# FFN 1's down projection by seven products of block sums in place of eight, in turns with up units, and three weight buffers for four

## The chip, the cores and the metric

The kernel runs on one core of a Trainium2 chip. A core has a matrix engine (PE, with its weight loads PEld), a vector engine (DVE), a scalar engine (ACT), a third elementwise engine (POOL), a queue that issues DMAs (SP), an on-chip memory in 128 partitions, and eight banks in which PE accumulates. Every engine works through its own instructions in the order of the program and waits for the others by semaphores. The metric is the device time of one execution in microseconds (us); less is better. A ratio is time after over time before.

## The reference

A decoder trunk of two layers over 256 tokens of width 2048, all in float32: pooling mixer, layer norm, gated FFN with a causal convolution of width 3, layer norm; then attention, layer norm, the second FFN (FFN 1, of layer 1), layer norm. What the change touches is the last line of the FFN:

```python
D_MODEL = 2048
SEQ = 256
D_FF = 128 * ((8 * D_MODEL // 3 + 127) // 128)   # 5504
...
def conv_ffn(h, w_up, conv_w, conv_b, w_down):
    """Gated MLP with causal depthwise conv (width 3) between up-projection and activation."""
    S = h.shape[1]
    u = h @ w_up
    up = jnp.pad(u, ((0, 0), (CONV_WIDTH - 1, 0), (0, 0)))
    c = conv_b + up[:, 0:S] * conv_w[0]
    for j in range(1, CONV_WIDTH):
        c = c + up[:, j:j + S] * conv_w[j]
    gate, val = jnp.split(c, 2, axis=-1)
    return (jax.nn.silu(gate) * val) @ w_down
...
        h = layer_norm(DEEPNORM_ALPHA * h + ff, ln2_g[i], ln2_b[i])
```

The output is the stream after the last layer norm, 256 x 2048.

## The kernel before, in words

**Units.** All weights pass through one list, `units`, of 364 entries. A unit is a tile of up to 512 rows by 512 columns of a weight (1 MB), the matmuls that use it, and what is to be done when its group is complete. `run_units` takes them in the list's order; the order of that list, and nothing else, sets the order of the program on every engine. For unit i it calls `ahead(i)`, then issues the unit's matmuls, then runs what is due (`later(n, fn)` puts a step off by n units), then the unit's own end (`post`).

**Loading and splitting.** `ahead(i)` issues loads on SP up to unit i + 5 (`do_load`; three buffers named `raw`), and splits up to unit i + `SP_AHEAD` (`do_split`). A split makes two rounded parts of a float32 weight: ACT casts `raw` to `wh` (L76), DVE subtracts to get `wl` (L77). Both have `SP_AHEAD + 1`, that is four, buffers. Each product is then three: high with high, high with low, low with high. The activations are split in the same way (`split_act`: L206 on ACT, L202 on DVE, in tiles called `xc`, `xp` or `g` with both parts).

**FFN 1.** Units 232 to 363. The inner width of 5504 is eleven pieces of 512 (the last of 384), q = 0 to 10. For each q there are four up units of the gate half and four of the value half (one for each 512 rows of the input). Most have 16 blocks, each with one matmul of 512 columns (L135) and one of 256 (L136). When a half's four units are done, `evac` copies and adds their sums (L512 on ACT, L513 on DVE), `conv` does the convolution (L521 on ACT, L525 on DVE), and the product of both halves becomes `g[q]` (L538, L539, L560, L206, L202). The down projection (`down`, `group_tm`) runs in chunks of q: 0 to 2, 3 to 5, 6 and 7, 8 to 10. A chunk is four groups, one for each 512 columns of the output, and in a group one unit for each q, of 24 matmuls of 512 columns (L165 to L167): two token halves, four blocks of 128 rows, three products. A group's two sums are added to the residual `ht` by DVE (L612). The up units of a chunk all come before its down units. `turns` swaps one pair of neighbours at each group's edge.

**What the change touches:** `SP_AHEAD` (L25), `do_load`, `do_split`, `ahead`, `run_units`, `group_tm`'s use for q below 8, `val_chain`, and the loop at the end of `ffn` (L590 to L593).

## Time and profile before

| | |
|---|---|
| time, three runs | 2086.20 to 2086.56 us, median 2086.37 |
| the profiled execution | 2086.31 us, of which the span of its instructions is 2084.5 |
| granted PE clock, mean | 0.998 |
| matmuls | 12992 |
| weights read | 380 MB at 183 GB/s |

The span is the time from the first to the last instruction. The profile gives busy time by engine, by group of instructions (line, engine, operation, tiles written and read, shape; then count, busy us, mean ns of one, and the idle time of the engine just before them with what ended it), the waits, the chain of work that ended last, and a timeline of single instructions. Matmuls are pipelined: a length in the timeline reaches beyond the next one's start, so what a matmul costs is read from start to start.

### The profile page before, as it was taken

What the parts mean: (1) busy time and instruction counts of PE and PEld (TensorE: products, weight loads), DVE (VectorE), ACT (ScalarE), POOL (GpSimd) and SP (SyncE); (2) the same over time, 40 slices, a digit from 0 to 9 for tenths busy, and PEclk for the clock granted to TensorE, in tenths of its full rate; (3) what the DMA queues carried; (4) which work ended last, traced back from release to release, by engine and by line L of the source; (5) the groups of instructions that cost most, each with busy time, mean ns of one, the idle gap of its engine ahead of it and who ended that gap; (6) DMA issues with size and microseconds to landing.
All of it is one profiled execution on the core that took longest, in us unless ns stands there. A gap on an engine that the chain in (4) does not pass through costs nothing.

```text
span 2084.5 us, 30605 instructions
## 1 busy us (share of the span) xinstructions
PE 2066.8 (99%) x12992; PEld 1861.9 (89%) x12992; DVE 1396.6 (67%) x1719; ACT 1027.4 (49%) x1142; POOL 11.4 (1%) x38
## 2 busy tenths in 40 slices
PE   9999999999999999999999999999999999999997
PEld 9999998888888888899888889999888888888886
DVE  6757787756756766778755666686646664665676
ACT  6445665345534535556544434475535543544552
POOL 2000000000000000000000000000000000000000
PEclk9999999999999999999999999999999999999999
DMA  8655465555565565554555455546555555555453
GB/s 263 211 184 186 156 204 180 202 182 185 179 202 182 182 202 172 187 188 162 182 172 176 164 173 185 182 143 202 189 195 182 183 197 186 183 193 190 153 202 131
DMA packets 195304, 384.09 MB, mean 184 GB/s; under 512 B 7022, under 2 KB 15876, under 8 KB 194912
## 3 DMA queue, kind: packets, MB, share of 16 engines
q1 hardware_dynamic: 194240, 381.71, 55.1%
q8 instruction: 101, 1.65, 0.3%
q0 software_dynamic: 928, 0.44, 0.1%
q14 instruction: 35, 0.29, 0.0%
HBM read 380.01 MB, written 2.10 MB: 183 GB/s over the span
## 4 chain that ended last, share of the span: by engine, by line
PE 98%; DVE 1%; DMA 0%; SPq 0%; ACT 0%; issue 0%
PE acc L135 35%; PE acc L136 18%; PE acc L139 9%; PE acc L140 9%; PE acc L138 9%; PE t L165 5%; PE t L166 5%; PE t L167 5%; PE s L720 0%; PE o L760 0%; DMA raw<-in_pool_w_in_dram 0%; PE pT L747 0%; PE s L719 0%; PE o L761 0%; PE hT L603 0%; DVE ht L669 0%
## 5 line engine op out<-in xcount | busy, mean ns | idle before, releaser
L77 DVE TENSOR_TENSOR wl<-raw,wh 128x2048 fp32r<-128x2048 f32 (+2 forms) x376 | 821.8, 2188 | 534.5 <-ACT wh L76 524.5
L76 ACT CAST wh<-raw 128x2048 fp32r<-128x2048 f32 (+2 forms) x376 | 685.6, 1827 | 609.6 <-PE acc L135 297.7
L135 PE MATMUL acc<-xc,wh 128*128 128x512 f32 x2624 | 924.1, 396 | 0.0
L136 PE MATMUL acc<-xc,wl 128*128 128x256 f32 x2624 | 736.2, 281 | 0.0
L135 PEld LDWEIGHTS acc<-xc,wh 128*128 128x128 f32 x2624 | 495.0, 189 | 116.6
L136 PEld LDWEIGHTS acc<-xc,wl 128*128 128x128 f32 x2624 | 494.9, 189 | 0.2
L135 PE MATMUL acc<-g,wh 128*128 128x512 f32 x512 | 179.9, 396 | 0.0
L138 PE MATMUL acc<-xc,wh 128*128 128x256 f32 x512 | 144.5, 282 | 1.6 <-ACT wh L76 1.6
L140 PE MATMUL acc<-xc,wl 128*128 128x256 f32 x512 | 144.4, 282 | 0.2 <-DVE wl L77 0.2
L139 PE MATMUL acc<-xc,wh 128*128 128x256 f32 x512 | 144.1, 281 | 0.0
L136 PE MATMUL acc<-g,wl 128*128 128x256 f32 x512 | 143.6, 280 | 0.0
L525 DVE SCALAR_TENSOR_TENSOR c<-u,cv,c 128x256 f32<-128x256 f32 x344 | 141.9, 480 | 0.6
L165 PE MATMUL t<-wh,g 128*128 128x512 f32 (+1 forms) x355 | 137.9, 388 | 0.0
L166 PE MATMUL t<-wl,g 128*128 128x512 f32 (+1 forms) x355 | 137.3, 387 | 0.0
L167 PE MATMUL t<-wh,g 128*128 128x512 f32 (+1 forms) x355 | 137.3, 387 | 0.0
L135 PEld LDWEIGHTS acc<-g,wh 128*128 128x128 f32 x512 | 96.6, 189 | 22.8
L139 PE MATMUL acc<-xp,wh 128*128 128x258 f32 x384 | 109.2, 284 | 0.0
L138 PE MATMUL acc<-xp,wh 128*128 128x258 f32 x384 | 109.0, 284 | 0.0
L140 PE MATMUL acc<-xp,wl 128*128 128x258 f32 x384 | 107.9, 281 | 0.0
L512 ACT COPY ut<-acc 128x256 f32<-128x256 f32 x140 | 51.6, 372 | 96.2 <-PE acc L136 96.0
L138 PEld LDWEIGHTS acc<-xc,wh 128*128 128x128 f32 x512 | 97.2, 190 | 1.8 <-ACT wh L76 1.8
L140 PEld LDWEIGHTS acc<-xc,wl 128*128 128x128 f32 x512 | 96.4, 188 | 0.5 <-DVE wl L77 0.4
(203 smaller groups left out, 2812.7 us busy)
## 6 DMA issues: line engine op xcount, KB each, us to landing
raw<-in_ffn_w_up_dram SPq DMA_DIRECT2D x160, 1024.0 KB, 5.1
raw<-in_ffn_w_down_dram SPq DMA_DIRECT2D x80, 1024.0 KB, 5.0
raw<-in_pool_w_out_dram SPq DMA_DIRECT2D x16, 1024.0 KB, 5.0
raw<-in_shared_w_k_dram SPq DMA_DIRECT2D x16, 1024.0 KB, 5.0
raw<-in_attn_w_q_dram SPq DMA_DIRECT2D x16, 1024.0 KB, 5.0
raw<-in_shared_w_v_dram SPq DMA_DIRECT2D x16, 1024.0 KB, 5.0
raw<-in_attn_w_o_dram SPq DMA_DIRECT2D x16, 1024.0 KB, 5.1
raw<-in_pool_w_in_dram SPq DMA_DIRECT2D x12, 1024.0 KB, 5.6
```

The costliest lines, as they stand in the source:

```text
L76: A.copy(wh[i][:, s], r[:, s])
L77: V.tensor_tensor(wl[i][:, s], r[:, s], wh[i][:, s].bitcast(F32), OP.subtract)
L135: PE.matmul(ps[m], h[:, k, c], q[:, k, :, :T], start=st, stop=False)
L136: PE.matmul(ps[m][:, :T], l[:, k, c], q[:, k, 0, :T], start=False, stop=sp)
L138: PE.matmul(ps[m][:, :n], h[:, k, c], q[:, k, 0, :n], start=st, stop=False)
L139: PE.matmul(ps[m][:, :n], h[:, k, c], q[:, k, 1, :n], start=False, stop=False)
L140: PE.matmul(ps[m][:, :n], l[:, k, c], q[:, k, 0, :n], start=False, stop=sp and not shifted)
L165: PE.matmul(to, xh, h[:, k, c], start=j == 0 and k == 0, stop=False)
L166: PE.matmul(to, xh, l[:, k, c], start=False, stop=False)
L167: PE.matmul(to, xl, h[:, k, c], start=False, stop=j == len(r0s) - 1 and k == nk - 1)
L512: A.copy(t, ps[m][:, T:])
L525: V.scalar_tensor_tensor(c[:, m, :], u[:, m, i:i + T], cv[:, i, j:j + 1], c[:, m, :], op0=OP.mult, op1=OP.add)
```

## The change

For layer 1 and q = 0 to 7, the product of a 512 by 512 weight tile with `g[q]` is now made as a 2 by 2 block product by seven block products instead of eight. The tile is cut in halves of rows and columns, `g[q]` in halves of its inner width and of tokens.

- **Two units for each tile.** `group_s` makes an "a" unit of three products and a "b" unit of four. Each product has two blocks of 128 rows and three matmuls of 256 columns: 18 and 24. Only a has a load; b has none and uses a's tile.
- **Splits.** For a, ACT casts three of the four blocks in two pieces (L103 of the new program), DVE subtracts (L105) and then forms four block sums in place in `raw` (L107 to L110). For b, ACT casts the four sums (L97) and DVE subtracts (L98). `split_order` puts the next unit that isn't a b ahead of each b in the order of splits; `ahead` splits in that order until all that are wanted are done.
- **Activation sums.** `val_chain` forms four sums of blocks of `g[q]` into `pend` (L289 to L292); `sums_tile` splits them into `xsum` (L295 on ACT, L296 on DVE) ahead of the chunk's first a.
- **Results.** Four banks hold the partial sums of a group; `s_post` combines them into `ht` with one copy on ACT (L819) and eight instructions on DVE (L820 to L828).
- **Order.** q = 0 and 1 up; then four turns, in which the eight pairs of q = a, a + 1 stand between the up units of the next two (in the last, three) q; then the down units of q = 8 to 10 as before.
- **Buffers.** `SP_AHEAD` is 2, so `wh` and `wl` have three buffers, in the whole kernel.

The diff, shortened to what it does:

```diff
 EPS = 1e-5
-SP_AHEAD = 3
+SP_AHEAD = 2
 WARM = 5
...
     state = {"loaded": 0, "split": 0, "done": 0}
+    is_split, order = set(), []
     raw, wh, wl = {}, {}, {}
...
         src = units[i][0]
+        if src is None:
+            return
         nk, n = src.shape[0] // P, src.shape[1]
...
     def do_split(i):
+        kind = units[i][3] if len(units[i]) > 3 else None
+        if kind is not None:
+            return split_sums(i, kind)
         r = raw.pop(i)
...
+    B1, B2, N1, N2 = slice(0, 2), slice(2, 4), slice(0, 256), slice(256, 512)
+    def split_sums(i, kind):
+        h = wh[i] = wp.tile([P, 4, 512], F32R, name=f"wh{i}", tag="wh")
+        l = wl[i] = wp.tile([P, 4, 512], F32R, name=f"wl{i}", tag="wl")
+        if kind == "b":
+            r = raw.pop(i - 1)
+            A.copy(h, r)
+            V.tensor_tensor(l, r, h.bitcast(F32), OP.subtract)
+            return
+        r = raw[i]
+        parts = [(slice(0, 4), N1), (B2, N2)]
+        for k, n in parts:
+            A.copy(h[:, k, n], r[:, k, n])
+        for k, n in parts:
+            V.tensor_tensor(l[:, k, n], r[:, k, n], h[:, k, n].bitcast(F32), OP.subtract)
+        r11, r12, r21, r22 = r[:, B1, N1], r[:, B1, N2], r[:, B2, N1], r[:, B2, N2]
+        V.tensor_tensor(r11, r12, r11, OP.subtract)
+        V.tensor_tensor(r12, r22, r12, OP.subtract)
+        V.tensor_tensor(r22, r22, r11, OP.subtract)
+        V.tensor_tensor(r21, r21, r22, OP.subtract)
+    def split_order():
+        held = None
+        for i, u in enumerate(units):
+            if len(u) > 3 and u[3] == "b":
+                held = i
+                continue
+            order.append(i)
+            if held is not None:
+                order.append(held)
+                held = None
+        if held is not None:
+            order.append(held)
     def ahead(i):
+        if not order:
+            split_order()
         while state["loaded"] < min(len(units), i + LD_AHEAD + 1):
...
         n = max(0, min(i - 1, SP_AHEAD) if i > 2 else 0)
-        while state["split"] < min(len(units), i + n + 1):
-            do_split(state["split"])
+        want = set(range(min(len(units), i + n + 1)))
+        while not want <= is_split:
+            j = order[state["split"]]
+            do_split(j)
+            is_split.add(j)
             state["split"] += 1
...
                 fn()
-            _, mm, post = units[i]
+            mm, post = units[i][1:3]
             mm(wh.pop(i), wl.pop(i))
...
+    def group_s(w, qs, c0, xq, xs, post):
+        ps = []
+        def mk(j, q, kind):
+            def go(h, l):
+                if j == 0 and kind == "a":
+                    ps.extend([bank(f"s{i}") for i in range(4)])
+                x, y = xq(q), xs(q)
+                last = j == len(qs) - 1
+                def a(k, t):
+                    return lambda hl, kk: x[:, k + kk, hl, t * P:t * P + P]
+                def sm(i):
+                    return lambda hl, kk: y[:, hl, i, kk, :]
+                if kind == "a":
+                    prods = [(a(0, 0), 0, N1, 0, 0, True, False), (a(2, 0), 2, N1, 2, 0, True, False),
+                             (sm(3), 2, N2, 0, 1, False, True)]
+                else:
+                    prods = [(a(2, 1), 2, N1, 1, 0, True, False), (sm(0), 0, N1, 1, 1, False, True),
+                             (sm(1), 2, N2, 3, 0, True, True), (sm(2), 0, N2, 2, 1, False, True)]
+                for left, k0, n, b, half, begins, ends in prods:
+                    to = ps[b][:, 256 * half:256 * half + 256]
+                    for kk in range(2):
+                        st, sp = begins and j == 0 and kk == 0, ends and last and kk == 1
+                        PE.matmul(to, left(0, kk), h[:, k0 + kk, n], start=st, stop=False)
+                        PE.matmul(to, left(0, kk), l[:, k0 + kk, n], start=False, stop=False)
+                        PE.matmul(to, left(1, kk), h[:, k0 + kk, n], start=False, stop=sp)
+            return go
+        for j, q in enumerate(qs):
+            units.append((w[512 * q:512 * q + 512, c0:c0 + 512], mk(j, q, "a"), None, "a"))
+            units.append((None, mk(j, q, "b"), (lambda: post(ps)) if j == len(qs) - 1 else None, "b"))
+    def sums(dst, src):
+        a11, a12, a21, a22 = (src[:, k:k + 2, t * P:t * P + P] for k, t in ((0, 0), (2, 0), (0, 1), (2, 1)))
+        V.tensor_tensor(dst[:, 0], a21, a22, OP.add)
+        V.tensor_tensor(dst[:, 1], dst[:, 0], a11, OP.subtract)
+        V.tensor_tensor(dst[:, 2], a11, a21, OP.subtract)
+        V.tensor_tensor(dst[:, 3], a12, dst[:, 1], OP.subtract)
+    def sums_split(dst, src):
+        A.copy(dst[:, 0], src)
+        V.tensor_tensor(dst[:, 1], src, dst[:, 0].bitcast(F32), OP.subtract)
     def quad_tile(nm):
...
         w_up, w_dn = ffn_w_up[lay], ffn_w_down[lay]
-        gq, gates = {}, {}
+        gq, gates, pend, xsum = {}, {}, {}, {}
+        seven = 8 if lay == 1 else 0
...
                     split_act(gq[q], s[:, :nb])
+                    if q < seven:
+                        pend[q] = (hp if q % 2 else lnp).tile([P, 4, 2, P], F32, name="pend", tag="h" if q % 2 else "sq")
+                        sums(pend[q], s)
...
-        for a, b in ((0, 3), (3, 6), (6, 8), (8, 11)):
-            for q in range(a, b):
+        if lay == 0:
+            for a, b in ((0, 3), (3, 6), (6, 8), (8, 11)):
+                for q in range(a, b):
+                    up(q)
+                down(range(a, b), b == 11)
+            return
+        def sums_tile(q):
+            xsum[q] = pools["ffn"].tile([P, 2, 4, 2, P], F32R, name="xsum", tag="xsum", bufs=2)
+            sums_split(xsum[q], pend.pop(q))
+        def down_s(qs):
+            mark = len(units)
+            for c in range(4):
+                group_s(w_dn, qs, 512 * c, lambda q: gq[q], lambda q: xsum[q], s_post(c))
+            got = units[mark:]
+            del units[mark:]
+            return [got[i:i + 2] for i in range(0, len(got), 2)]
+        def ups(qs):
+            mark = len(units)
+            for q in qs:
                 up(q)
-            down(range(a, b), b == 11)
+            got = units[mark:]
+            del units[mark:]
+            return got
+        units.extend(ups((0, 1)))
+        for a in (0, 2, 4, 6):
+            us, ds = ups((a + 2, a + 3) if a < 6 else (8, 9, 10)), down_s((a, a + 1))
+            at = (4, 5, 7, 8, 10, 11, 13, 14) if a < 6 else (4, 5, 8, 9, 12, 13, 16, 17)
+            for i, u in enumerate(us):
+                if i == at[0] - 1:
+                    before.setdefault(len(units), []).extend([lambda q=q: sums_tile(q) for q in (a, a + 1)])
+                units.append(u)
+                for k, d in zip(at, ds):
+                    if k == i + 1:
+                        units.extend(d)
+        down(range(8, 11), True)
...
                 store(cc, 1)
+        return post
+    def s_post(c):
+        def post(ps):
+            fp = pools["ffn"]
+            y = HT[c]
+            p1, u2, u3 = (fp.tile([P, 256], F32, name=nm, tag="s3", bufs=3) for nm in ("p1", "u2", "u3"))
+            A.copy(p1, ps[0][:, :256])
+            V.tensor_tensor(y[:, 0, :], y[:, 0, :], ps[0], OP.add)
+            V.tensor_tensor(u2, p1, ps[3][:, :256], OP.add)
+            V.tensor_tensor(y[:, 0, :256], y[:, 0, :256], ps[2][:, :256], OP.add)
+            V.tensor_tensor(u3, u2, ps[2][:, 256:], OP.add)
+            V.tensor_tensor(u2, u2, ps[1][:, 256:], OP.add)
+            V.tensor_tensor(y[:, 1, :], y[:, 1, :], ps[1], OP.add)
+            V.tensor_tensor(y[:, 0, 256:], y[:, 0, 256:], u2, OP.add)
+            y2 = y[:, 1, :].rearrange("p (a n) -> p a n", a=2)
+            V.tensor_tensor(y2, y2, u3.unsqueeze(1).to_broadcast([P, 2, 256]), OP.add)
         return post
...
```

Where instructions stand now. **First place: ACT's casts in the first turn.** Before, in a down chunk, units 259 to 263 (the number behind `wh` and `raw` is the unit's; the one behind the underscore only counts tiles):

```order
L76 CAST wh259_14005<-raw259_13900 128x2048
L206 CAST g_14036<-c_13847 128x4x256
L76 CAST wh260_14041<-raw260_13938 128x2048
L76 CAST wh261_14071<-raw261_14003 128x2048
L76 CAST wh262_14103<-raw262_14039 128x2048
L76 CAST wh263_14135<-raw263_14069 128x2048
```

After the change, units 256 to 261, of which 257, 258 and 261 are up units, 259 is an a, and 256 and 260 are b units, which read the `raw` tile of 255 and 259:

```order
L84 CAST wh257_13900<-raw257_13823 128x2048
L97 CAST wh256_13904<-raw255_13693 128x2048
L84 CAST wh258_13964<-raw258_13860 128x2048
L819 COPY p1_13992<-s0_13825 128x256
L103 CAST wh259_14006<-raw259_13898 128x4x256
L103 CAST wh259_14006<-raw259_13898 128x2x256
L84 CAST wh261_14048<-raw261_13962 128x2048
L97 CAST wh260_14052<-raw259_13898 128x2048
```

The casts no longer stand in the order of the units: 257 is ahead of 256, and 261 ahead of 260. PE runs 256 to 261 in the order of their numbers.

**Second place: DVE in the first turn, around the second pair.** Before, the subtractions of units 255 to 258, with a convolution and a gate's product between them:

```order
L77 TENSOR_TENSOR wl255_13808<-raw255_13689,wh255_13807 128x2048
L525 SCALAR_TENSOR_TENSOR c_13847<-u_13791,cv1_733,c_13847 128x256 x8
L77 TENSOR_TENSOR wl256_13863<-raw256_13740,wh256_13862 128x2048
L539 TENSOR_TENSOR c_13847<-u_13791,c_13847 128x1024
L77 TENSOR_TENSOR wl257_13903<-raw257_13805,wh257_13902 128x2048
L77 TENSOR_TENSOR wl258_13941<-raw258_13860,wh258_13940 128x2048
```

After, from a gate's convolution to the split of unit 258; 255 is an a, 256 its b, 257 and 258 up units:

```order
L626 SCALAR_TENSOR_TENSOR c_13847<-u_13809,cv1_729,c_13847 128x256 x8
L105 TENSOR_TENSOR wl255_13863<-raw255_13693,wh255_13862 128x4x256
L105 TENSOR_TENSOR wl255_13863<-raw255_13693,wh255_13862 128x2x256
L107 TENSOR_TENSOR raw255_13693<-raw255_13693 128x2x256
L108 TENSOR_TENSOR raw255_13693<-raw255_13693 128x2x256
L109 TENSOR_TENSOR raw255_13693<-raw255_13693 128x2x256
L110 TENSOR_TENSOR raw255_13693<-raw255_13693 128x2x256
L640 TENSOR_TENSOR c_13847<-u_13809,c_13847 128x1024
L85 TENSOR_TENSOR wl257_13901<-raw257_13823,wh257_13900 128x2048
L98 TENSOR_TENSOR wl256_13905<-raw255_13693,wh256_13904 128x2048
L85 TENSOR_TENSOR wl258_13965<-raw258_13860,wh258_13964 128x2048
```

Between the convolution and the split of the next up unit now stand two subtractions and four block sums of the a, and the b's own subtraction comes behind the up unit's.

**Third place: DVE in the first turn, behind a value half's end** (numbers left out but for the weight tiles; the first row is the subtraction of b unit 263, `wl_14247` is that of up unit 265):

```order
L98 TENSOR_TENSOR wl_14155<-raw_14004,wh_14154 128x2048
L595 MEMSET u 128x4x2
L614 TENSOR_TENSOR u<-acc,ut 128x256 x4
L626 SCALAR_TENSOR_TENSOR c<-u,cv_729,c 128x256 x8
L661 TENSOR_TENSOR c<-c 128x1024
L302 TENSOR_TENSOR g<-c,g 128x4x256
L289 TENSOR_TENSOR pend<-c 128x256
L290 TENSOR_TENSOR pend<-pend,c 128x256
L291 TENSOR_TENSOR pend<-c 128x256
L292 TENSOR_TENSOR pend<-c,pend 128x256
L85 TENSOR_TENSOR wl_14247<-raw_14112,wh_14246 128x2048
L820 TENSOR_TENSOR ht<-ht,s_14090 128x512
```

The first row of `s_post` is the last shown; seven more follow, and then the split of a unit 266, of up unit 268 and of b unit 267. New in this piece are the four rows of `pend` and `s_post`; before, the subtractions of the next units followed the low part of `g` directly.

## Prediction

> **What bounds the kernel now.** I read the page's busy shares and its chain of work that ended last, then the waits of PE, then busy time by stage, then single rows of the timeline for what one step costs.
>
> ```profile
> span 2084.5 us, 30605 instructions
> PE 2066.8 (99%) x12992; PEld 1861.9 (89%) x12992; DVE 1396.6 (67%) x1719; ACT 1027.4 (49%) x1142; POOL 11.4 (1%) x38
> PE 98%; DVE 1%; DMA 0%; SPq 0%; ACT 0%; issue 0%
> ```
>
> The first two lines are the span and each engine's busy time, the third is the chain's share by engine. PE is on the chain for 98% of the span, so a microsecond of matmuls less is a microsecond less, as long as nothing makes PE wait. The next view, who waited for whom, kept to PE, has four rows of which this is the longest:
>
> ```profile
> PE acc L138 <- ACT wh L76: 1.6, 1, 1.6
> ```
>
> It is at the start. After that PE never waits: every split weight tile (`wh`, `wl`) is ready ahead of its unit. What the other engines have to spare in FFN 1 shows in two stretches, 24 up units, then 12 down units (columns: stretch, its length, busy time of PE, PEld, DVE, ACT, POOL, clock, DMA share, GB/s):
>
> ```profile
> 1549.00:1684.00 135.00, 135.00 (x770) 117.98 (x769) 87.36 (x101) 68.39 (x73) 0.00 (x0) 1.00 0.57 187
> 1684.00:1751.00 67.00, 67.00 (x290) 54.16 (x290) 38.42 (x31) 26.16 (x19) 0.00 (x0) 1.00 0.56 188
> ```
>
> DVE is busy 65% and 57% of them. So there is room on DVE, but not without end, and the change spends it.
>
> **The change part by part. 1: fewer products.** Matmuls of the timeline (start in us, length, engine, line, tiles, shape):
>
> ```profile
> 1311.17 0.28 PE L138 MATMUL acc<-o,wh 128*128 128x256 f32 x1
> ...
> 1339.69 0.29 PE L138 MATMUL acc<-xp,wh 128*128 128x258 f32 x1
> ...
> 1683.60 0.39 PE L165 MATMUL t<-wh,g 128*128 128x512 f32 x1
> ...
> 1750.57 0.39 PE L135 MATMUL acc<-xc,wh 128*128 128x512 f32 x1
> ```
>
> The first two rows bound five units of 48 matmuls of 256 columns: 28.52 us / 240 = 0.1188 us each. The other two bound twelve down units of 24 matmuls of 512 columns: 66.97 / 288 = 0.2325 us. An old down unit is 24 x 0.2325 = 5.58 us; the new pair is 18 matmuls ("a", 2.14 us) and 24 ("b", 2.85 us) of 256 columns, 42 x 0.1188 = 4.99 us. That is 0.59 us less for each of 32: **-18.9 us**. An up unit is 16 x (0.2325 + 0.1188) = 5.62 us; there are as many as before.
>
> **2: the wait for "b".** The three slots of `wh` are taken in the order of the splits, and that order is up, a, next up, b. In the rows of ACT shown with the change (258, 259, 261, 260) b's tile therefore takes the slot of the up unit that runs just before a: b's cast can't begin before a does. What follows then has rows in the trace before, where a cast also waited for the end of a unit (1627.40 is the next unit's first matmul):
>
> ```profile
> 1627.40 0.39 PE L135 MATMUL acc<-xc,wh 128*128 128x512 f32 x1
> ...
> 1627.49 1.91 ACT L76 CAST wh<-raw 128x2048 fp32r<-128x2048 f32 x1 [2.23 <-PE acc L135]
> ...
> 1629.42 2.29 DVE L77 TENSOR_TENSOR wl<-raw,wh 128x2048 fp32r<-128x2048 f32 x1 [1.98 <-ACT wh L76]
> ```
>
> From that matmul to the end of the subtraction are 4.31 us. Unit a covers 2.14 of them, and b's second matmul reads `wl`: PE stands about 2.2 us at every pair, with DVE free. The four-slot kernel hid the same 4.31 us behind three whole units. 32 x 2.2 = **+70.4 us**. No other work lies between a and b on PE, so nothing covers it.
>
> **3: more work on DVE.** What it costs, by rows of like shape, grouped and then in time:
>
> ```profile
> L77 DVE TENSOR_TENSOR wl<-raw,wh 128x2048 fp32r<-128x2048 f32 x111 | 254.3, 2291 | 184.3 <-ACT wh L76 183.7
> L513 DVE TENSOR_TENSOR u<-acc,ut 128x256 f32<-128x256 f32 x70 | 26.3, 417 | 18.1 <-ACT ut L512 18.1
> L612 DVE TENSOR_TENSOR ht<-ht,t 128x512 f32<-128x512 f32 x31 | 21.2, 683 | 14.7 <-PE t L167 14.7
> L202 DVE TENSOR_TENSOR g<-c,g 128x1024 fp32r<-128x1024 f32 x10 | 12.3, 1227 | 11.2 <-ACT g L206 11.2
> ```
>
> ```profile
> 1641.07 2.29 DVE L77 TENSOR_TENSOR wl<-raw,wh 128x2048 fp32r<-128x2048 f32 x1 [1.38 <-ACT wh L76]
> 1643.27 3.26 DVE L525 SCALAR_TENSOR_TENSOR c<-u,cv,c 128x256 f32<-128x256 f32 x8
> 1646.45 2.29 DVE L77 TENSOR_TENSOR wl<-raw,wh 128x2048 fp32r<-128x2048 f32 x1
> ...
> 2066.05 0.69 DVE L648 TENSOR_TENSOR ht<-ht,g 128x512 f32<-128x512 f32 x1 [0.88 <-ACT ht L645]
> 2066.77 0.69 DVE L649 TENSOR_TENSOR ht<-ht,b 128x512 f32<-128x512 f32 x1
> 2067.38 0.68 DVE L648 TENSOR_TENSOR ht<-ht,g 128x512 f32<-128x512 f32 x1
> ```
>
> An instruction begins before the last one ends, so I count from start to start: a whole split 2.20, a convolution of four blocks 3.18, a 512-column step 0.72 where it needs the one before (L649) and 0.61 where not. By the same 0.07 to 0.09 of overlap, 1024 columns (1227 ns) are 1.15 and 256 columns (417 ns) 0.35, or about 0.42 where they depend. The new steps then are: split of a, 1.15 + 0.61 + four dependent block sums of 512 = 4.6; split of b, 2.2; `s_post`, three of 512 and five of 256 = 3.7; four activation sums 1.7; the low part of a sum 1.15. No row shows subtractions in place on strided blocks. Ends for their 0.72: 0.61 (start to start of independent ones) and 1.15 (the next larger shape); I take L649, the nearest.
>
> A turn of 16 up units and 8 pairs is 16 x 5.62 + 8 x 4.99 = 129.8 us of PE. DVE has 16 x 2.2 + 8 x 6.8 + 4 groups x (4 x 0.35 + 3.18) + products and low parts of g 2 x 1.15 + 2 x 3.4 + sums 2 x 1.7 + 2 x 1.15 + 4 x 3.7 = 138 us. The 3.4 hold a wait for ACT's cast, 24.1 us over 22 times:
>
> ```profile
> DVE g L202 <- ACT g L206: 24.1, 22, 1.1
> ```
>
> So DVE needs more than the bare 129.8, but less than the 129.8 + 8 x 2.2 = 147.4 that part 2 makes of it. On average it fits; it is in bursts that it doesn't. I follow its queue, which is strictly in order, from the end of one b's subtraction to the next b's:
> - First pair: the third product of a reads `xsum`, whose low part stands behind b's subtraction in DVE's queue. PE stands 4.31 + 1.15 - 1.43 (two products) = 4.0 instead of 2.2: +1.8.
> - Second pair (the rows of DVE shown with the change): low parts 2.3, evacuation 1.4, convolution 3.18, split of a 4.6, gate product 1.15, split of the next up 2.2, split of b 2.2 = 17.0 us. From the same point PE has the rest of the first pair's a and b, an up unit and an a: 1.2 + 0.7 + 2.85 + 5.62 + 2.14 = 12.5. It stands 4.5: +2.3.
> - Fifth pair, behind a value group's end: evacuation 1.4, convolution 3.18, g 3.4, sums 1.7, split 2.2, `s_post` 3.7, split of a 4.6, two splits 4.4 = 24.6 us, against b, two ups and a on PE, 2.85 + 11.24 + 2.14 = 16.2. It stands 8.4 in two pieces, the first before the second up unit: +6.2.
> - The other five pairs find DVE done in time: 2.2 each.
>
> That is 10.3 us a turn beyond part 2. There are four turns (the last has 24 up units, and the same kinds of bursts): **+41 us**.
>
> **4: three buffers elsewhere.** A split made three units ahead is now made two ahead, at the same place in DVE's queue. Of 376 splits of the trace before, 246 were waited for by a DVE that had nothing else to do (us in total, times, longest):
>
> ```profile
> DVE wl L77 <- ACT wh L76: 524.5, 246, 5.4
> ```
>
> Those end as in part 2, 4.3 us after their buffer's release, and two units give 11.2: no cost. It is short at the two places where layer norm's work stands in the queue; there the subtraction in the slot of the unit after next ends too late for the unit itself:
>
> ```profile
> 266.38 0.28 PE L138 MATMUL acc<-xc,wh 128*128 128x256 f32 x1
> ...
> 266.92 2.29 DVE L77 TENSOR_TENSOR wl<-raw,wh 128x2048 fp32r<-128x2048 f32 x1
> ...
> 1387.69 0.28 PE L138 MATMUL acc<-xc,wh 128*128 128x256 f32 x1
> ...
> 1387.98 2.28 DVE L77 TENSOR_TENSOR wl<-raw,wh 128x2048 fp32r<-128x2048 f32 x1
> ```
>
> The unit that starts at 266.38 would get its `wl` at 269.21, the one at 1387.69 at 1390.26: 2.8 + 2.6 = **+5.4 us**. (Ends: nothing, if DVE's own waits shrink there; 11, if ACT's casts come late as well.)
>
> At nothing I cost ACT's added casts and copies (it is idle half the time, and b's cast is counted above), and the DMAs: SP's queue holds the same loads in the same order,
>
> ```profile
> raw<-in_ffn_w_down_dram SPq DMA_DIRECT2D x80, 1024.0 KB, 5.0
> ```
>
> and a load takes 5.0 us. A pair's raw tile is held until b's subtraction, but the load that follows into it is wanted two or three units later, 10 us or more; should that cover go in the fifth pair's burst, it is 2 us a turn.
>
> **Sum.** -18.9 + 70.4 + 41 + 5.4 = +98 us on the profiled execution's 2086.3 (span 2084.5 and 1.8 around it), which is within 0.1 of the median of 2086.37: **2184 us**.
>
> **The rivals.** *DVE's bursts are absorbed* (cheaper block sums, or slack that I don't see): parts 1, 2 and 4 alone, 2086 - 18.9 + 70.4 + 5.4 = 2143. For it: the sum over a turn fits. Against it: the order within the queue.
>
> *The clock falls in the waits.* In the trace it fell once, after PE's last matmul:
>
> ```profile
> 2070.03 0.28 PE L167 MATMUL t<-wh,g 128*128 128x256 f32 x1
> ...
> 2072.00:2078.00 6.00, 0.00 (x0) 0.00 (x0) 5.79 (x14) 0.29 (x1) 0.00 (x0) 0.69 0.11 44
> 2078.00:2084.00 6.00, 0.00 (x0) 0.00 (x0) 3.23 (x5) 0.00 (x0) 0.00 (x0) 0.50 0.45 175
> ```
>
> PE ends at 2070.3; a mean of 0.69 over six microseconds is 3.7 us at half clock, so it fell at 2074.3, 4.0 us after. Four waits in a turn are of 4.0 to 4.5 us, right at that. If each costs about 4 us at half clock, 2 us of work are lost: 16 x 2 = 32, some of which waits for DVE anyway: 2200 to 2216. The Trainium skill, "TensorE: Matmul & The Clock Gate", Part 1 on the HAM clock gate, speaks against the change in the same way: one idle window of about 3.4 us halves the clock, and about 3.4 us of activity bring it back. By its figure the long waits would nearly all do so, 16 x 1.7 = 27 us, an estimate, and the waits of 2.2 us would not. One fall in the tail can't tell the two figures apart.
>
> *Faster.* If b's cast were released one unit earlier, 4.31 us would hide behind an up unit and a (7.8 us), part 2 would be zero, and with DVE's 138 pressed under 130 the time would be 2086 - 18.9 + 5.4 = 2073. It decides from the point at which b's split ends within a's 2.14 us. The slot order speaks against it at every pair; only a release of the slot before the up unit's last matmul could make it so.
>
> *DVE costs more than I took*, with block sums nearer 1.15 than 0.72: 1.7 us more for each pair, all of it in the bursts and some elsewhere: 2200 to 2240.
>
> **How the numbers follow.** My forecast, 2184 (2160 to 2207): 0.6. Bursts absorbed, 2130 to 2160: 0.18. Clock or dearer DVE, 2207 to 2245: 0.18. Faster: 0.03; within 0.2%, which is about what a measurement of this kernel can tell from no change: 0.01. The range for 8 in 10 is 2138 to 2222: it leaves out the faster case and the ends of the two slow ones. Slower by over 0.2%: 0.96.
>
> **What would show it.** In the changed kernel's waits of PE, `s1` (b) waiting for `wl` of L98 should lead with some 32 waits and 70 us or more, most near 2.2 us; next `acc` and `s0` after the bursts. `s` matmuls should start every 0.119 us. If b's waits are much under 2 us, part 2 is wrong; if PE waits little beyond them, part 3 is; if the page's clock row shows 8s in the last third, the clock rival holds. DVE's share should come to some 75% of the span.

## The result, and the profile after

| | before | after |
|---|---|---|
| time, median of the runs | 2086.28 us (2085.94 to 2086.56) | 2219.51 us (2216.95 to 2223.23) |
| after / before | | 1.064 [1.0627, 1.0652] |
| profiled execution, its span | 2086.31, 2084.5 us | 2216.95, 2214.8 us |

The change makes the kernel 133 us slower. The page of the changed kernel, the lines that answer to those of before (span, busy times, the granted clock in 40 slices, the chain that ended last):

```profile
span 2214.8 us, 32282 instructions
PE 2101.1 (95%) x13568; PEld 1919.0 (87%) x13568; DVE 1596.8 (72%) x2055; ACT 1085.5 (49%) x1230; POOL 11.4 (1%) x38
PEclk9999999999999999999999999999998998999999
PE 80%; DVE 14%; ACT 4%; issue 2%; DMA 0%; SPq 0%; ACTq 0%; DVEq 0%
```

PE's share of the chain falls from 98% to 80%, and DVE and ACT come onto it. PE is busy 34 us *longer* than before, though the change takes 18.9 us of matmuls away. Both have to be explained. The waits of PE, one row for each awaited line:

```profile
PE s L278 <- DVE wl L98: 47.2, 22, 3.2
PE s L277 <- ACT wh L97: 18.1, 6, 5.2
PE s L278 <- DVE u L595: 11.7, 6, 1.9
PE s L279 <- DVE xsum L296: 8.1, 4, 2.0
PE s L277 <- ACT xsum L295: 4.9, 4, 1.5
PE acc L190 <- DVE wl L85: 4.3, 5, 1.3
```

L97 and L98 are b's cast and subtraction. The third row names a memset of 0.07 us that stands behind b's subtraction in DVE's queue; its six waits are of the same 1.94 us and belong to L98. Why b's split comes so late shows at the pair whose a begins at 1499.02, in the rows of PE, ACT and DVE:

```profile
1499.02 0.28 PE L277 MATMUL s<-wh,g 128*128 128x256 f32 x1
...
1499.15 1.91 ACT L97 CAST wh<-raw 128x2048 fp32r<-128x2048 f32 x1 [3.75 <-PE acc L185]
...
1501.09 2.29 DVE L98 TENSOR_TENSOR wl<-raw,wh 128x2048 fp32r<-128x2048 f32 x1 [3.36 <-ACT wh L97]
```

ACT stood idle for 3.75 us until the matmuls of the up unit ahead of a gave the slot free, and DVE is done 4.36 us after a's first matmul. Of the 30 casts of b before which ACT stood idle, 25 were released by an up unit (L185, L186) and five by DVE's last block sum (L110). The stretch of one turn, from the first pair of the second turn to that of the third:

```profile
1627.31:1790.98 163.67, 142.21 (x850) 128.45 (x849) 134.33 (x172) 77.45 (x82) 0.00 (x0) 0.93 0.46 155
```

A turn takes 163.7 us. PE stands for 163.67 - 142.21 = 21.5 of them, and is at work for 142.2, where its matmuls at full speed are 129.8. The granted clock, 0.93, says most of why. One b, matmul by matmul:

```profile
1501.14 0.36 PE L277 MATMUL s<-wh,g 128*128 128x256 f32 x1
1503.44 0.38 PE L278 MATMUL s<-wl,g 128*128 128x256 f32 x1 [1.94 <-DVE wl L98]
1503.66 0.28 PE L279 MATMUL s<-wh,g 128*128 128x256 f32 x1
...
1504.13 0.41 PE L277 MATMUL s<-wh,xsum 128*128 128x256 f32 x1
1504.34 0.42 PE L278 MATMUL s<-wl,xsum 128*128 128x256 f32 x1
```

```profile
1500.71:1504.12 3.41, 1.47 (x12) 1.26 (x11) 3.03 (x2) 1.91 (x3) 0.00 (x0) 1.00 0.44 170
1504.12:1507.53 3.41, 3.41 (x18) 3.41 (x17) 3.31 (x6) 0.00 (x0) 0.00 (x0) 0.50 0.89 286
```

The wait is 1.94 us. The first step behind it takes 0.22 us (1503.44 to 1503.66) where others take 0.12. Then, 0.7 us *after* PE had begun again, the clock halves for 3.41 us, and a matmul takes 0.21 us. So each wait costs more than it lasts.

### The profile page after: what moved, and what is told of

The parts are those of the page before. It is cut to its first block, busy times and chain, and to the rows that moved or that the text cites. A ratio compares the mean times of both kernels' runs of the same rounds, so it can differ in the third digit from the quotient of the medians.

```text
span 2214.8 us, 32282 instructions
## 1 busy us (share of the span) xinstructions
PE 2101.1 (95%) x13568; PEld 1919.0 (87%) x13568; DVE 1596.8 (72%) x2055; ACT 1085.5 (49%) x1230; POOL 11.4 (1%) x38
## 4 chain that ended last, share of the span: by engine, by line
PE 80%; DVE 14%; ACT 4%; issue 2%; DMA 0%; SPq 0%; ACTq 0%; DVEq 0%
PE acc L185 31%; PE acc L186 16%; PE acc L190 7%; PE acc L189 7%; PE acc L188 7%; DVE wl L98 3%; DVE wl L85 3%; PE t L216 2%; PE t L215 2%; PE t L217 2%; DVE c L626 2%; ACT wh L97 2%; PE s L278 2%; PE s L279 1%; PE s L277 1%
## 5 line engine op out<-in xcount | busy, mean ns | idle before, releaser
L85 DVE TENSOR_TENSOR wl<-raw,wh 128x2048 fp32r<-128x2048 f32 (+2 forms) x344 | 747.9, 2177 | 404.6 <-ACT wh L84 396.4
L185 PE MATMUL acc<-xc,wh 128*128 128x512 f32 x2624 | 927.2, 396 | 0.0
L84 ACT CAST wh<-raw 128x2048 fp32r<-128x2048 f32 (+2 forms) x344 | 624.3, 1819 | 531.4 <-PE acc L185 255.5
L186 PE MATMUL acc<-xc,wl 128*128 128x256 f32 x2624 | 737.1, 281 | 1.5 <-DVE wl L85 1.5
L185 PEld LDWEIGHTS acc<-xc,wh 128*128 128x128 f32 x2624 | 496.7, 189 | 115.4
L186 PEld LDWEIGHTS acc<-xc,wl 128*128 128x128 f32 x2624 | 496.3, 189 | 1.9 <-DVE wl L85 1.8
L185 PE MATMUL acc<-g,wh 128*128 128x512 f32 x512 | 179.9, 396 | 0.0
L186 PE MATMUL acc<-g,wl 128*128 128x256 f32 x512 | 143.6, 280 | 0.0
L278 PE MATMUL s<-wl,g 128*128 128x256 f32 x192 | 61.1, 318 | 59.9 <-DVE wl L98 47.2
L185 PEld LDWEIGHTS acc<-g,wh 128*128 128x128 f32 x512 | 96.7, 189 | 22.8
L98 DVE TENSOR_TENSOR wl<-raw,wh 128x2048 fp32r<-128x2048 f32 x32 | 73.2, 2289 | 59.2 <-ACT wh L97 59.2
L97 ACT CAST wh<-raw 128x2048 fp32r<-128x2048 f32 x32 | 61.1, 1908 | 108.7 <-PE acc L185 76.8
L622 ACT ACTIVATE c<-u,cv 128x256 f32<-128x256 f32 x172 | 89.7, 596 | 16.7 <-DVE u L614 16.7
```

What stands on the lines that cost most here:

```text
L84: A.copy(wh[i][:, s], r[:, s])
L85: V.tensor_tensor(wl[i][:, s], r[:, s], wh[i][:, s].bitcast(F32), OP.subtract)
L97: A.copy(h, r)
L98: V.tensor_tensor(l, r, h.bitcast(F32), OP.subtract)
L185: PE.matmul(ps[m], h[:, k, c], q[:, k, :, :T], start=st, stop=False)
L186: PE.matmul(ps[m][:, :T], l[:, k, c], q[:, k, 0, :T], start=False, stop=sp)
```

## The experiments

"In-run half clock" is the sum of the stretches that the trace's clock record shows at half clock ahead of PE's end; in the changed kernel it is 102 us in 23 stretches. "Turn" is the stretch shown above, found in each kernel at its own place. Ratios are to the kernel before, timed on the same chip.

**Three buffers alone**, in the kernel before.

```diff
-SP_AHEAD = 3
+SP_AHEAD = 2
```

> The kernel before with SP_AHEAD of 2, that is three buffers for wh and wl, and nothing else of the change. Theory A: waits only where each FFN begins, 1.29 + 0.88 and 1.11 + 0.84 us in the changed kernel's trace, no window at half clock: 2089.5 to 2092 us. Rival: two units ahead are short all over FFN 1 too, and part of the waits of the changed kernel come from that: over 2095.

2091.53 us, 1.0026 [1.0017, 1.0036]. PE waits where part 4 put it:

```profile
PE acc L140 <- DVE wl L77: 4.4, 5, 1.3
```

Forecast in part 4: +5.4; measured against the 2086.14 of the kernel before, timed with it: +5.4.

**Splits in the order of the list.**

```diff
     def split_order():
-        held = None
-        for i, u in enumerate(units):
...
+        order.extend(range(len(units)))
```

> The changed kernel with one part undone: weight tiles are split in the order of the units (up, a, b, up) and no longer with the next up unit ahead of b. Theory A (b's cast waits for the slot of the up unit just before a; the bursts on DVE come on top; the clock falls behind waits of about 1.9 us): b now takes the slot of the unit one further back, its 4.31 us lie behind an up unit and a, so the waits for L98 and L97, 65 us in the changed kernel, fall under 10, and with them most of the 102 us at half clock. 2100 to 2130 us. Rival B (DVE's amount of work makes the waits, whatever the order): the waits only move to other lines, 2190 to 2220.

2181.01 us, 1.0454 [1.0438, 1.0469]: between both. PE's waits (PE's line numbers are 10 lower here):

```profile
PE s L268 <- DVE wl L98: 23.4, 16, 1.9
PE s L267 <- ACT wh L97: 22.7, 10, 4.1
PE acc L176 <- DVE wl L85: 12.4, 10, 2.1
```

Under the names of L97, L98 and the memset b waited 77.0 us in the changed kernel; here it is 46.8. But now up units (`acc L176`) wait as well, since with three slots some unit always gets a slot that comes free late. So order alone doesn't settle it: there is a slot too few, or DVE is too slow, and this run can't say which.

**Needless matmuls in b's wait.** Four, then fourteen, of 256 columns at the head of b, into a half bank that isn't read; they add work and no result.

```diff
+                else:
+                    for _ in range(4):
+                        PE.matmul(ps[3][:, 256:512], a(0, 0)(0, 0), held[j][:, 0, N1], start=j == 0, stop=j == 0)
```

> The changed kernel plus four needless matmuls of 256 columns (0.48 us together, into the unused half of a bank, never read) at the head of every b, where PE waits anyway: the 128 of them are added work. In the trace of the changed kernel the windows of 3.41 us with 1.88 us or more of idle PE are followed by 3.41 us at half clock, those with 1.79 or less are not. Theory A (idle time in a window makes the clock fall, and that costs PE time): the common wait shrinks from 1.94 to 1.46 us, the clock stays up behind five of eight pairs, 30 half-clock windows become 10 to 16, and added matmuls make the kernel faster: 2180 to 2202 us. Rival C (the low clock falls into waiting time and costs nothing): 2215 to 2225.

> As the run with four needless matmuls, but 14 at the head of every b (1.66 us): the common wait shrinks to 0.3 us. Theory A: the second pair's wait of 2.76 us falls under the limit too, 4 to 10 half-clock windows are left (those of the waits in a and behind the value half), 2172 to 2198 us; where a wait is shorter than the 1.66 us of filling, the filling is paid. Rival C: 2219 to 2240.

2211.70 us, 1.06 [1.0584, 1.0616], and 2211.98 us, 1.0603 [1.0587, 1.0618]. Each lies between its two theories and in neither range. With four, the common wait falls to 1.46 to 1.54 us, none of these is followed by half clock, and the in-run half clock goes from 102 to 65 us, which is 19 times 3.41 us where 10 to 16 were forecast; with fourteen it is 68. Yet the time falls by 7.8 us only. Under L97, L98 and the memset b's waits fall by 12.1 us (77.0 to 64.9) for 15.4 us of needless matmuls (128 x 0.12), and other waits grow. The edit has a part in this that I hadn't meant: the needless matmuls read a's tile, so they hold its slot longer: 11 of ACT's casts with four, and 17 with fourteen, began only when they were done. What that costs isn't shown, so these runs don't price the clock by itself.

**POOL takes the four block sums.**

```diff
-        V.tensor_tensor(r11, r12, r11, OP.subtract)
+        nc.gpsimd.tensor_tensor(r11, r12, r11, OP.subtract)
...
```

> The four block sums of a weight tile go from DVE to POOL, which is idle in this stage; nothing else changes. DVE is rid of 8 x 2.9 = 23 us a turn, 93 us in all. Theory A (the prediction: b's slot wait of about 2 us a pair stands by itself, the bursts of DVE at pairs 1, 2 and 5 come on top): the bursts go, the slot waits stay: 41 us and what hangs on them off, 2165 to 2182, and PE's waits for L98 all near 1.9 us. Theory B (one chain through DVE sets the whole turn, and each stand of PE is only where it shows): more than that, 2110 to 2150. Theory C (POOL takes longer for a sum than DVE, over 2 us each, and b's cast now waits for it): 2215 to 2300.

2286.69 us, 1.0958 [1.0942, 1.0975]: theory C. POOL's groups (busy time, mean ns of one):

```profile
L108 POOL TENSOR_TENSOR raw<-raw 128x512 f32<-128x512 f32 x32 | 64.3, 2011 | 2.5
...
L109 POOL TENSOR_TENSOR raw<-raw 128x512 f32<-128x512 f32 x32 | 46.3, 1446 | 2.5
```

1.4 to 2.0 us a sum, against DVE's 0.69, and b's cast waits for all four. This run says nothing about DVE's load, which I had meant it to.

**b multiplies by a's tiles.** No product waits for b's split, and ACT and DVE keep their work.

```diff
         if kind == "b":
-            r = raw.pop(i - 1)
-            A.copy(h, r)
-            V.tensor_tensor(l, r, h.bitcast(F32), OP.subtract)
+            wh[i], wl[i] = wh[i - 1], wl[i - 1]
+            r = raw.pop(i - 1)
+            A.copy(r, r)
+            V.tensor_tensor(r, r, r, OP.subtract)
...
-                             (sm(1), 2, N2, 3, 0, True, True), (sm(2), 0, N2, 2, 1, False, True)]
+                             (sm(1), 2, N2, 3, 0, True, True), (sm(2), 2, N2, 2, 1, False, True)]
```

> b multiplies by the split tiles of a in place of its own, and its cast and subtraction are done within the raw tile, where nothing on PE reads them: ACT and DVE keep their work, PE never waits for b's split, and one tile of three stays held through a and b. (b's products are left out in so far as they use the wrong weights, as many and as large.) Theory A (slot wait 2.2 a pair, bursts beside it): 2219 less 70 and the half clock that follows these waits, 2115 to 2145. Theory B (DVE has too much work for the turn, 138 us against 129.8, and sets the time whatever b waits for): 8 us a turn over PE, 2086 - 19 + 5 + 33 = 2105, so 2095 to 2115, with PE's idle time now at the up units. Theory C (as with the splits in the order of the list, the wait only moves to the next up unit): 2165 to 2185.

**The same without b's split and the block sums.**

```diff
-            A.copy(r, r)
-            V.tensor_tensor(r, r, r, OP.subtract)
...
-        V.tensor_tensor(r11, r12, r11, OP.subtract)
-        V.tensor_tensor(r12, r22, r12, OP.subtract)
-        V.tensor_tensor(r22, r22, r11, OP.subtract)
-        V.tensor_tensor(r21, r21, r22, OP.subtract)
```

> As the run before it, and b's cast and subtraction and the four block sums are left out: DVE loses 8 x 5.1 = 41 us a turn, ACT 15. What is left of the change is the 42 matmuls of 256 columns a pair, the split of a, the activation sums, the evacuation by s_post and the three buffers. Theory A (products -18.9, three buffers +5.4, the rest hidden once DVE has room): 2073, so 2070 to 2080. Theory B (the evacuations and activation sums at the ends of pairs hold PE up by themselves, or the products are not as cheap): 2086 or more.

2106.02 us, 1.0094 [1.0077, 1.0111], and 2075.13 us, 0.9945 [0.993, 0.996]: theory B of the one and theory A of the other, though in the first PE's waits are more at the a units than at the up units that theory B had named. The turn, in this order:

```profile
1602.97:1742.10 139.13, 132.89 (x851) 120.12 (x849) 132.69 (x173) 76.13 (x83) 0.00 (x0) 0.99 0.53 182
```

```profile
1595.90:1726.06 130.16, 130.05 (x851) 118.50 (x849) 95.82 (x133) 63.08 (x74) 0.00 (x0) 1.00 0.58 194
```

Without the slot wait DVE is busy 132.69 of 139.13 us, 95%, and the rest is mostly short waits for ACT, so DVE sets the turn; the prediction had counted 138 us for it, some waits for ACT included. With its two extra loads gone the turn is 130.16, against 129.8 of bare matmuls. So the products are as cheap as forecast, and activation sums and `s_post` hide.

**The slot wait alone: no block sums.** In the changed kernel, only the four subtractions on `raw` of the last diff are left out.

> The four block sums of a weight tile are left out (the products use the blocks as loaded); b's cast and subtraction stay, in their slot, so that PE waits for them as in the changed kernel. DVE has 23 us a turn less, 115 for 129.8 of PE. Theory A (the prediction's part 2: the slot wait stands by itself, near 2.2 us a pair, PE idle long enough to lose some clock behind it): 2143 by the prediction's parts 1, 2 and 4, with the clock up to 2165; PE's waits for L98 32 times near 1.9 us. Theory B (the slot wait costs only when DVE is short as well): 2080 to 2115.

2184.25 us, 1.0484 [1.0461, 1.0506]: above both theories. PE's waits in one turn (1620 to 1777), and the turn:

```profile
PE s L273 <- DVE wl L98: 10.8, 6, 1.9
PE s L273 <- DVE wl L105: 2.1, 1, 2.1
PE s L274 <- DVE xsum L291: 2.0, 1, 2.0
PE s L273 <- DVE u L590: 1.9, 1, 1.9
PE s L272 <- ACT xsum L290: 1.5, 1, 1.5
```

```profile
1618.19:1775.05 156.86, 138.50 (x850) 125.09 (x849) 113.46 (x140) 77.54 (x82) 0.00 (x0) 0.96 0.48 161
```

The waits are as theory A has them, some 2 us at each pair with DVE at ease: 18.4 us a turn. But PE is at work 138.5 us for what took 130.05 in the run before: 8.4 us more. Those are slower matmuls at half clock (58 us of it in the run) and the slow first steps behind waits. My upper end, 2165, had too little for them.

**The same with four needless matmuls.** The edit is that of the filled runs.

> The run without block sums, with four needless matmuls of 256 columns (0.48 us) at the head of each b, into a half bank that is not read. b's subtraction ends when it did, so the wait behind them should be 1.94 - 0.48 = 1.46 us, and the sum of both as long as before. Theory A (PE idle for 1.9 of 3.41 us halves the clock for the next 3.41, and with DVE at ease each such stretch costs about half its length): the half clock falls from 58 us ahead of the tail to under 25, and the time from 2184 to 2145-2165. Theory B (as in the changed kernel, PE at full clock only waits longer): 2175 to 2187.

2182.41 us, 1.0458 [1.0441, 1.0475]: theory A missed, and the time is in theory B's range. No wait of 1.46 to 1.50 us is followed by half clock, but longer and double waits (1.46 and 2.02 us close together near 1623) remain, and the in-run half clock falls from 58 to 41 us, not under 25. Of 17 us of half clock some 44% is lost work (a step of 0.213 against 0.119), 7.5 us; the time fell by 1.8, less than the scatter of these runs (2183.0 to 2193.2 and 2178.9 to 2183.9). The rest went into waiting, as in the first filled run: b's needless and idle time together came to 45.5 + 15.4 = 60.9 us, where its idle time had been 58.3. Here too a's slot is held longer.

**Four products in a, three in b.** A change that computes the same: the first block sum is split into the unused quarter of a's tiles and its product moves into a; b's split comes in two pieces.

```diff
         if kind == "b":
...
+            for k, n in [(slice(0, 4), N2), (B2, N1)]:
+                A.copy(h[:, k, n], r[:, k, n])
+                V.tensor_tensor(l[:, k, n], r[:, k, n], h[:, k, n].bitcast(F32), OP.subtract)
...
         V.tensor_tensor(r11, r12, r11, OP.subtract)
+        A.copy(h[:, B1, N2], r11)
...
+        V.tensor_tensor(l[:, B1, N2], r11, h[:, B1, N2].bitcast(F32), OP.subtract)
```

> One of b's four products goes into a, with its block split into the quarter of a's tiles that nothing uses: a has 24 matmuls (2.85 us), b 18. b's cast and subtraction come in two pieces, 1024 columns first. From a's first matmul b's first subtraction should end after 0.1 + 1.0 + 0.1 + 1.2 = 2.4 us, its second by 3.2, needed at 2.85 + 1.4: no wait in the same three slots. The same sums and as much DVE work, two instructions more a pair. Theory A (slot wait 2.2 us is what costs most, DVE's 138 us against 129.8 the rest): near the run in which b read a's tiles, 2105 to 2130. Theory B (casts and subtractions are late because DVE and ACT are, not because the slot is): 2160 or more.

2172.33 us, 1.0414 [1.0399, 1.043]: 47 us off the change, and in theory B's range. Sixteen of the waits for b's subtraction remain, now 2.1 us in the mean (here L98 is b's cast, L99 its subtraction):

```profile
PE s L281 <- DVE wl L99: 33.0, 16, 2.5
PE s L280 <- ACT wh L98: 9.8, 7, 4.1
```

The slot wait is gone from half of the pairs; in the others the pieces come late because ACT and DVE have other work in front of them. In one such pair DVE goes from a's subtractions through the block sums and an up unit's split to b's pieces without a pause, from 1722.04 to 1731.10.

**The same with POOL's help**, for the last block sum and the activation sums.

```diff
-        V.tensor_tensor(r21, r21, r22, OP.subtract)
+        nc.gpsimd.tensor_tensor(r21, r21, r22, OP.subtract)
...
-        V.tensor_tensor(dst[:, 0], a21, a22, OP.add)
+        nc.gpsimd.tensor_tensor(dst[:, 0], a21, a22, OP.add)
...
```

> As the run before it, and POOL takes the last of the four block sums, which only b's last product reads, and the four activation sums of each chunk. DVE is rid of 32 x 0.7 and 32 x 0.4 = 35 us; by the run with all four sums on POOL (1.9 us a sum; DVE lost 31 us to 230 us of POOL) some 13 come back. Theory A (DVE's load sets the time once the slot wait is gone): 20 us below the run before it, 2085 to 2110. Theory B (POOL's 2 to 3 us stand in the chain from a's split to b's last product): no better than the run before it, up to 2140.

2176.09 us, 1.0426 [1.0411, 1.0442]: no gain over the run before it, which is theory B's reason, though its upper end of 2140 was too low. DVE's busy time went from 1599.2 to 1591.0 us where 35 us of work were taken from it.

**b from a's tiles, block sums on POOL.** Both edits shown above together.

> The run in which b multiplies by a's tiles (no slot wait, 2106), with the four block sums on POOL, where all of them took 7.6 us a pair; b's cast and subtraction within the raw tile wait for POOL, and no product waits for these. DVE is rid of 93 us, and gives back some 31 by the earlier run with POOL. Theory A (DVE's load was all that was left): 2075 to 2088, so seven products could just pay with a slot more. Theory B (POOL's 7.6 us stand ahead of b's subtraction, behind which DVE's queue waits in order): 2106 or more.

2228.36 us, 1.068 [1.0664, 1.0696]: theory B. One pair in time, by the timelines of DVE, POOL and ACT:

```profile
1668.99 3.38 DVE L85 TENSOR_TENSOR wl<-raw,wh 128x2048 fp32r<-128x2048 f32 x1
...
1674.96 1.29 POOL L111 TENSOR_TENSOR raw<-raw 128x512 f32<-128x512 f32 x1
...
1676.29 1.91 ACT L96 COPY raw<-raw 128x2048 f32<-128x2048 f32 x1 [7.58 <-POOL raw L111]
...
1678.23 2.29 DVE L97 TENSOR_TENSOR raw<-raw 128x2048 f32<-128x2048 f32 x1 [5.85 <-ACT raw L96]
```

ACT waits 7.6 us for POOL's last sum, DVE 5.9 for ACT, and since DVE's queue is in order, the evacuations and splits behind that subtraction wait too, though no product reads it.

None of the kernels with all of the change's work beats the kernel before. The most that one could reach by these runs is the time of the run without b's split and the block sums: 2075 us, 11 below.

## Why it came out so

The sign and the range held, the range by 2.5 us only; the time was 35.5 us above the forecast, and not in the case to which I had given 0.6 (2160 to 2207) but in that of the clock or dearer DVE (2207 to 2245, 0.18). The wait behind b's late slot, the main term, is there as forecast. What failed is the clock, which I had left out of the sum, and with it part of the price of DVE's bursts. The runs split the 133 us into three, each a difference of two medians:

| step | forecast | measured |
|---|---|---|
| products and three buffers (before, to the run without b's split and block sums) | -18.9 + 5.4 = -13.5 | -11.2 |
| b's split and the block sums as work for DVE (that run, to b from a's tiles) | +41 as bursts | +30.9 |
| PE's wait for b's split (that, to the changed kernel) | +70.4 | +113.5 |

The last row is all that b's own split tiles bring: the late slot, one tile more for three slots at each pair, and whatever else holds the split up. That the late slot does this by itself, with DVE at ease, is shown by the run without block sums, 109 us above the one without b's split. But the steps don't add up in any order: with four products in a and three in b, the longer cover of b's split gave back 47 us, for DVE's full queue then made half of the pairs wait.

**Parts 1 and 4, products and buffers: right.** The turn of 130.16 and the run with three buffers show both terms, to within 2.3 us in sum.

**Part 2, b's wait: right in place and length, short in what it costs.** The cast in the late slot, then the subtraction, then PE: the typical wait is 1.94 us for 2.2 forecast. Over a turn PE's idle time grows by 21.5 - 6.2 = 15.2 us from the run without the slot wait to the changed kernel; the forecast was 17.6. But the same two rows have PE at work for 132.89 and 142.21 us, 9.3 us more for the same matmuls. That is the clock and the slow first steps, over four such turns 37 us beside 61 of waiting, 98 of the 113.5; nearly all the rest is in the last turn, which has 24 up units (from its first pair to PE's end it is 37.7 us longer than in the run without the wait, the first three turns 24.5 to 25.1 each).

**Part 3, DVE's bursts: the right load and length, too large a price.** The load of 138 us a turn is what the run without the slot wait shows (139.1, of which DVE is busy 132.7). With the slot wait, taking the block sums away gives 163.67 - 156.86 = 6.8 us a turn and 35.3 us in all; without it, b's split and the sums cost 30.9. Both are under 41. The places were right and PE's stands were shorter: in the second turn of the changed kernel pair 1 stands 3.5 us (forecast 4.0), pair 2 2.7 (4.5), pair 5 5.5 in three pieces (8.4). PE's idle time of 21.5 us a turn stands against 27.9 forecast. It was not DVE's queue that I had too long. From behind one b's subtraction to behind the next b's, for pairs 2 and 5 (first row, last subtraction, next row):

```profile
1631.59 2.35 DVE L296 TENSOR_TENSOR xsum<-pend,xsum 128x1024 fp32r<-128x1024 f32 x2
...
1646.27 2.28 DVE L98 TENSOR_TENSOR wl<-raw,wh 128x2048 fp32r<-128x2048 f32 x1
1648.47 2.28 DVE L85 TENSOR_TENSOR wl<-raw,wh 128x2048 fp32r<-128x2048 f32 x1
```

```profile
1681.32 0.41 DVE L614 TENSOR_TENSOR u<-acc,ut 128x256 f32<-128x256 f32 x1
...
1703.31 2.28 DVE L98 TENSOR_TENSOR wl<-raw,wh 128x2048 fp32r<-128x2048 f32 x1
1705.51 1.82 DVE L105 TENSOR_TENSOR wl<-raw,wh 128x1024 fp32r<-128x1024 f32 x2
```

DVE takes 16.9 us and 24.2, where my walk had 17.0 and 24.6. PE's side was wrong: it was to be 12.5 and 16.2 us and is 16.9 - 2.7 = 14.2 and 24.2 - 5.5 = 18.7, mostly because the clock had halved behind the wait before (at 1633.83 and 1681.61). Slow matmuls stood where I had PE waiting.

**The clock rival: near in size (32 us forecast, 37 by part 2), wrong in its trigger.** This is the step that failed. I put its onset at stands of 4.0 us, from the one fall in the tail, so only 16 long stands of pairs 1, 2 and 5 would have cost 2 us each, and I gave it as a case of its own at 0.18 with dearer DVE. The page's clock row has an 8 in two slices, both in the last third, which was the sign that I had named for this rival. In the trace it is there behind most of the common waits (12 of the 18 single ones of 1.93 to 2.02 us): the 1.94 us shown above halve the clock. The sum with it in its place, by the turn: 129.8 + 21.5 idle + 12.4 = 163.7, where the forecast was 129.8 + 27.9 = 157.7. So two errors, 6.4 us too much idle time and 12.4 us of slow work left out, partly cancel, and as part 3 shows, much of the first comes from the second. That the total stayed in the range owes something to this. The Trainium skill, "TensorE: Matmul & The Clock Gate", Part 1, has it that one idle window of about 3.4 us halves the clock; I took from it that waits of 2.2 us would not; the trace disagrees, with 1.94 of 3.41 us.

**Absorbed bursts and faster** are out: PE stands beyond the slot wait, and the slot comes late in nearly every pair, as forecast. Of the marks that I had named, L98 leads the waits, with 22 under its own name and six more under the memset's, 58.9 us, for 32 and 70 us forecast; `s` matmuls step by 0.119 us at full clock; DVE's share is 72% for 75%.

**What stays open** is how the clock and DVE share the loss in the changed kernel itself. Filling b's wait took 37 us of half clock away and gave 7.8 us, with a's slot held longer as well; the slow matmuls are partly cover for DVE's work, so the 12.4 us a turn are not what a steady clock would give back.

## What to carry to other kernels

Before a unit is cut in two, follow the buffer ring: if the second half's tile takes the slot of the unit just ahead of the first half, its whole chain (here 4.3 us of cast and subtraction) stands behind a cover of half a unit, at every pair. Count the helper engine's queue over a whole turn against the shorter main work: here PE lost 4.7 us of 134.5 a turn while DVE's work rose to 138, and the turn took 139 even with no slot wait. And price a wait on PE at its length, plus the slow start, plus what a halved clock takes from the work behind it.

## What the runs showed of the hardware

- **Half clock behind short waits.** The clock record moves on a fixed grid of 3.41 us. In the changed kernel each stretch of the grid in which PE was idle for 1.88 us or more is followed by one at half clock, and none with 1.79 or less, unless the clock was low already. In the run without block sums the same 1.94 us, when a grid line cuts them, do nothing, and with the needless matmuls neither do 1.50:

```profile
1577.24:1580.65 3.41, 2.47 (x21) 2.27 (x19) 2.78 (x2) 2.95 (x2) 0.00 (x0) 1.00 0.25 38
1580.65:1584.06 3.41, 2.41 (x20) 2.41 (x21) 3.41 (x3) 1.13 (x2) 0.00 (x0) 1.00 0.98 342
1584.06:1587.47 3.41, 3.41 (x22) 3.07 (x22) 3.38 (x9) 1.91 (x1) 0.00 (x0) 1.00 1.05 406
```

```profile
1499.53:1502.94 3.41, 1.91 (x17) 1.71 (x15) 2.34 (x2) 2.60 (x3) 0.00 (x0) 1.00 0.65 252
1502.94:1506.35 3.41, 3.40 (x26) 3.33 (x27) 1.69 (x2) 0.37 (x1) 0.00 (x0) 1.00 0.66 196
```

  The line is not sharp: in the run without block sums one stretch with 1.83 us had no fall behind it, and one with 1.68 had. In the changed kernel a grid line cuts pair 2's wait of 2.7 us in the first three turns, and no half clock follows it there.
- **A matmul behind a wait starts slowly:** 0.22 us to the next one in place of 0.12.
- **POOL is slow at elementwise work, and DVE pays for it.** A sum of 512 columns took it 1.4 to 2.0 us, against 0.69 on DVE. With the same 1927 instructions DVE was busy 1535.6 us beside 230 us of POOL's sums and 1513.1 without; a whole split took 3.18 us at a place where POOL was at work, for 2.29.
